# Attention heads on two-bank PSUM tiles, with 1/sum multiplied into the output

## The chip, the core and the metric

The kernel runs on one core of a Trainium2 chip. Its engines, each with its own in-order instruction stream, are named as the profile names them: PE (TensorE: matmuls; PEld is its weight loads), DVE (VectorE), ACT (ScalarE), POOL (GpSimd) and SP (SyncE, whose queue issues the weight loads). The metric is the device time of one execution in microseconds, the median of several runs; lower is better.

## The reference

A block stack of depth 2 on 256 latent tokens and 256 context tokens, width 1024, in float32. Each layer is: half a feed-forward, a mixer, half a feed-forward, each with an RMS norm that is modulated (scaled, shifted, and gated on its output) by vectors computed from a conditioning vector. Layer 0's mixer is a short convolution, layer 1's is attention with 8 query heads over 2 key/value heads; only the latent tokens attend, to all 512 tokens. Cut to what matters here:

```python
def _attend(q, k, v):
    s = jnp.einsum('bqhgd,bkhd->bhgqk', q, k).astype(jnp.float32) * (ATTN_HEAD_DIM ** -0.5)
    p = jax.nn.softmax(s, axis=-1).astype(v.dtype)
    return jnp.einsum('bhgqk,bkhd->bqhgd', p, v)

def reference(...):
    lat, cx = x, ctx
    for i in range(DEPTH):
        ...
        mod = (jax.nn.silu(c) @ mod_w[i] + mod_b[i]).reshape(bsz, 3, 3, 1, D_MODEL)
        modc = (jax.nn.silu(c_ctx) @ mod_w[i] + mod_b[i]).reshape(3, 3, D_MODEL)
        lat = lat + 0.5 * mod[:, 0, 2] * _swiglu(_modulate(lat, norm_g[i, 0], mod[:, 0, 0], mod[:, 0, 1]), ffn_w13[i, 0], ffn_w2[i, 0])
        ...
            y, yc = _gqa_mixer(h, hc, ctx_out, attn_w_qkv[j], attn_q_g[j], attn_k_g[j], attn_w_o[j], cos, sin)
        ...
        lat = lat + mod[:, 1, 2] * y
        ...
    return lat
```

## The kernel before

**Exactness.** A float32 product is made of three matmuls: every operand is split into a high part that TensorE takes at full rate and a low rest. `split` is two instructions, a copy to the high part on ACT (L98) and a subtraction for the low part on DVE (L99), and `mm3` issues high x high, high x low and low x high (L122, L123, L124). So every weight tile of 128x1024 costs one ACT copy, called wh in the profile, and one DVE subtraction, wl.

**Layout and stages.** Activations lie with the channels on the 128 partitions and 512 tokens along the free axis. The stages run in this order: a feed-forward, the convolution, a feed-forward (layer 0); a feed-forward, the attention, a feed-forward (layer 1). The first three feed-forwards work on all 512 tokens and make their hidden tiles in block pairs: `Pair` forms a 2x2 block product with seven products instead of eight (`head`, `five`, `six`, `seven`, `four`), from sums of weight blocks that DVE forms and splits. There are 54 such pairs. The last feed-forward has 256 tokens only and no pairs. Each is followed by projections (`project`) with the second weight matrix.

**Modulation.** Besides the first two, the modulation vectors are computed on DVE: 224 units, each one custom instruction (L142, output called junk) that multiplies 128x1024 weights with the conditioning vector and sums, and a short read of the accumulator. The weights come in loads of 1 MB (modT) into the three buffers wr that all weights share, through SP's queue. `tick(n)` releases n more units at that place of the program; `mod_ready` forces those that are due. Ticks of 6 stand in each step of the convolution, smaller ones in the projections, and 2 for each head.

**Attention.** After the projections of q and k with norm and rotary embedding, `v_proj(0..3)` make v for four tiles of 128 tokens. Then, for each of 8 heads: `scores` (two query tiles of 128, each in a PSUM bank of its own, psc: three matmuls of 512 columns, a maximum over the row on DVE L1042, its scaled negative nb L1044, the exponential e on ACT L1050 that sums into sm, the reciprocal r L1054, and the scaled probabilities pn = e * r on GpSimd L1058); `turn` (eight transposes on TensorE L1067 into two banks pt, each split to pth and ptl); `mix` (12 matmuls into pav, then the split to a). PSUM has eight banks: two pools, psm with six and pss with two, are open for the whole kernel.

The heads are written two ahead:

```python
    pns, pts = {0: scores(0)}, {}
    v_proj(2)
    v_proj(3)
    pns[1] = scores(1)
    for hd in range(HEADS):
        if hd + 2 < HEADS:
            pns[hd + 2] = scores(hd + 2)
        pts[hd] = turn(pns.pop(hd))
        if hd:
            mix(hd - 1, pts.pop(hd - 1))
        tick(2)
    mix(HEADS - 1, pts.pop(HEADS - 1))
```

Then wo is projected (py, 192 matmuls of 256 columns), finished into x (L446) with squares and sums for the next norm, and the last feed-forward begins (first matmul pg). Between them stand the norm's sums ss (L237, L248), ri (L246), t (L256) and hh (L266).

**What sets the order.** A scheduler places all instructions when the program is built: it may move them within an engine's stream against the written order, by its own priorities. On the chip the order on each engine is fixed, and each instruction waits for the semaphores of what it reads or overwrites.

Of the kernel before, what the change touches and what calls it, by code (L numbers as in the profile page):

```python
# [16 lines left out]
P = 128  # L17
# [24 lines left out]
def hybrid_kernel(ctx: ExitStack, tc: tile.TileContext, a: dict, out: bass.AP):  # L42
# [7 lines left out]
    psm = ctx.enter_context(tc.tile_pool(name="psm", bufs=6, space=bass.MemoryType.PSUM))  # L50
    pss = ctx.enter_context(tc.tile_pool(name="pss", bufs=2, space=bass.MemoryType.PSUM))
# [8 lines left out]
    def psum(s="ps"):  # L60
        return psm.tile([P, T2], F32, tag="mm", name=nm(s))

    def psmall(s="pq"):
        return pss.tile([P, T2], F32, tag="sm", name=nm(s))
# [468 lines left out]
    class Pair:  # L533
# [66 lines left out]
        def seven(self):  # L600
            self.prod(self.p, "S3", "T3", False)
            nc.vector.tensor_tensor(
                out=self.u[:, S:], in0=self.p, in1=self.gm[:, S:], op=ALU.add
            )

# [232 lines left out]
    for m in range(KT):  # L838
# [36 lines left out]
        tick(6)  # L875
# [29 lines left out]
    pqs = pss.tile([P, T2], F32, tag="sm", name="pqs")  # L905
# [126 lines left out]

    def scores(hd):
        kv = hd // (HEADS // KVH)
        r_ = []
        for qt in range(2):
            o = (hd % 2) * S + qt * P
            ps = psum("psc")
            mm3(ps, tuple(t[:, o : o + P] for t in qs[hd // 2]), ks[kv], True, True)
            ci = hd * 2 + qt  # L1040
            mx = ap.tile([P, 1], F32, name=nm("mx"), tag="mx", bufs=4)
            nc.vector.reduce_max(mx, ps, axis=AX.X)  # L1042
            nb = ap.tile([P, 1], F32, name=nm("nb"), tag="nb", bufs=4)
            nc.vector.tensor_scalar(  # L1044
                out=nb, in0=mx, scalar1=scq[:, ci : ci + 1], scalar2=-1.0,
                op0=ALU.mult, op1=ALU.mult,
            )
            e = tp.tile([P, T2], F32, name=nm("e"), tag="sg", bufs=3)
            sm = ap.tile([P, 1], F32, name=nm("sm"), tag="smx", bufs=4)
            nc.scalar.activation(  # L1050
                out=e, in_=ps, func=AF.Exp, scale=scq[:, ci : ci + 1], bias=nb, accum_out=sm
            )
            r = ap.tile([P, 1], F32, name=nm("r"), tag="r", bufs=4)
            nc.vector.reciprocal(r, sm)  # L1054
            if qt == 0:
                pn2 = hot("pn", F32)
            pn = pn2[:, qt * T2 : qt * T2 + T2]
            nc.gpsimd.tensor_scalar(out=pn, in0=e, scalar1=r, scalar2=None, op0=ALU.mult)  # L1058
            r_.append(pn)
        return r_  # L1060

    def turn(pn):
        pth, ptl = (hot(t).rearrange("p (b q) -> p b q", q=S) for t in ("pth", "ptl"))
        for qt in range(2):
            pt = psum("pt")
            for kt in range(4):
                nc.tensor.transpose(  # L1067
                    pt[:, kt * P : kt * P + P], pn[qt][:, kt * P : kt * P + P], ident
                )
            split(  # L1070
                pth[:, :, qt * P : qt * P + P], ptl[:, :, qt * P : qt * P + P],
                pt.rearrange("p (k q) -> p k q", k=4),
            )
        return pth, ptl
# [3 lines left out]
    def mix(hd, pt):  # L1078
# [4 lines left out]
        po = psum("pav")  # L1083
        for kt in range(4):
            vw = tuple(t[:, kv * P : kv * P + P] for t in vs[kt])
            mm3(po[:, :S], vw, (pt[0][:, kt, :], pt[1][:, kt, :]), kt == 0, kt == 3)
        o = (hd % 2) * S
        ah, al = (t[:, o : o + S] for t in at[-1])
        split(ah, al, po[:, :S])
        aos.append((ah, al))  # L1090

    pns, pts = {0: scores(0)}, {}
    v_proj(2)
    v_proj(3)
# [99 lines left out]
```

## Time and profile before

| | us |
|---|---|
| time, median of 3 runs (lowest to highest) | 1596.06 (1595.92 to 1598.62) |
| span of the profiled execution | 1599.4 |
| PE busy | 1572.9 (98%) |
| DVE busy | 1304.2 (82%) |
| ACT busy | 718.6 (45%) |
| POOL busy | 29.7 (2%) |

The profiled execution has no time of its own beside its span. The span is 3.3 us over the median of the runs. Busy times are of one execution; a wait is put down to the semaphore that came last.

### The profile page before, as it was taken

To read this page: it belongs to the slowest core of one execution; us is meant where nothing else is said; L and a number is where in the kernel's file an instruction comes from. 1 tells how busy PE (TensorE), PEld (TensorE's weight loads), DVE (VectorE), ACT (ScalarE), POOL (GpSimd) and SP (SyncE) were. 2 spreads that over 40 slices of the span, in tenths; PEclk is the share of its full clock that TensorE was granted. 3 is DMA by queue.
4 is the path that set the end of the run, shared out by engine and by line. 5 is a ranking of instruction groups with operands and counts; after the bars stand their busy time and mean duration, and the time that the engine had idled before them with its cause. 6 is when DMAs were issued, how large, how long until landed. Compare 5 with 4: busy or idle time off the path is not lost.

```text
span 1599.4 us, 25805 instructions
## 1 busy us (share of the span) xinstructions
PE 1572.9 (98%) x10674; PEld 1452.2 (91%) x10674; DVE 1304.2 (82%) x1984; ACT 718.6 (45%) x1103; POOL 29.7 (2%) x20
## 2 busy tenths in 40 slices
PE   8999999999999999999999999999999998899999
PEld 6788998998888899999899899889899897899999
DVE  4778788879998879799798899898797799965554
ACT  5632452544322366335245375245254455554443
POOL 0000000000000000000000000000000005100000
PEclk9999999999999999999999999999999999989999
DMA  8455234234565422453443423452432554755462
GB/s 312 173 185 187 103 106 175 103 117 160 184 220 198 162 80 83 155 185 100 139 145 106 174 78 108 175 191 96 155 132 97 181 199 150 261 189 187 167 201 104
DMA packets 38422, 248.79 MB, mean 156 GB/s; under 512 B 5280, under 2 KB 7072, under 8 KB 12448
## 3 DMA queue, kind: packets, MB, share of 16 engines
q1 hardware_dynamic: 35712, 245.38, 44.0%
q10 hardware_dynamic: 2592, 1.76, 0.4%
q8 instruction: 83, 1.36, 0.3%
q14 instruction: 35, 0.29, 0.1%
HBM read 244.77 MB, written 1.05 MB: 154 GB/s over the span
## 4 chain that ended last, share of the span: by engine, by line
PE 87%; DVE 7%; DMA 3%; ACT 1%; issue 1%; POOL 0%; DVEq 0%; ACTq 0%; SPq 0%; POOLq 0%
PE py L122 8%; PE py L123 8%; PE py L124 8%; PE p L123 6%; PE p L122 6%; PE p L124 6%; PE q L124 5%; PE q L122 5%; PE q L123 5%; PE pg L122 3%; PE pg L123 3%; PE pg L124 3%; PE pu L124 3%; PE pu L123 3%; PE pu L122 3%; DVE junk L142 2%
## 5 line engine op out<-in xcount | busy, mean ns | idle before, releaser
L98 ACT ACTIVATE wh<-wr 128x1024 fp32r<-128x1024 f32 (+2 forms) x276 | 276.4, 1014 | 401.1 <-PE py L123 111.3
L99 DVE TENSOR_TENSOR wl<-wr,wh 128x1024 fp32r<-128x1024 f32 (+2 forms) x276 | 320.0, 1167 | 96.5 <-ACT wh L98 95.9
L142 DVE CUSTOM_DVE_ANT_0 junk<-wr,scbc,modb 128x1024 bf16<-128x1024 f32 x224 | 287.0, 1281 | 38.9 <-DMA wr<-in_modT 36.3
L122 PE MATMUL py<-gh,wh 128*128 128x512 f32 (+1 forms) x746 | 263.2, 353 | 0.0
L123 PE MATMUL py<-gl,wh 128*128 128x512 f32 (+1 forms) x746 | 263.1, 353 | 0.0
L124 PE MATMUL py<-gh,wl 128*128 128x512 f32 (+1 forms) x746 | 262.8, 352 | 0.0
L124 PEld LDWEIGHTS py<-gh,wl 128*128 128x128 f32 x746 | 141.1, 189 | 19.1
L122 PEld LDWEIGHTS py<-gh,wh 128*128 128x128 f32 x746 | 141.2, 189 | 18.5
L123 PEld LDWEIGHTS py<-gl,wh 128*128 128x128 f32 x746 | 141.2, 189 | 18.1
L99 DVE TENSOR_TENSOR wl<-ws,wh 128x1024 fp32r<-128x1024 f32 x108 | 131.8, 1224 | 29.1 <-ACT wh L98 28.9
L98 ACT ACTIVATE wh<-ws 128x1024 fp32r<-128x1024 f32 x108 | 113.5, 1058 | 68.0 <-PE p L123 35.5
L124 PE MATMUL p<-th,wl 128*128 128x256 f32 x432 | 122.2, 283 | 0.0
L123 PE MATMUL p<-tl,wh 128*128 128x256 f32 x432 | 122.2, 283 | 0.0
L122 PE MATMUL p<-th,wh 128*128 128x256 f32 x432 | 122.2, 283 | 0.0
L446 DVE SCALAR_TENSOR_TENSOR x<-py,G,x 128x256 f32<-128x256 f32 x168 | 74.1, 479 | 21.9 <-PE py L124 21.4
L122 PE MATMUL q<-bh,wh 128*128 128x256 f32 x320 | 90.6, 283 | 0.0
L123 PE MATMUL q<-bl,wh 128*128 128x256 f32 x320 | 90.6, 283 | 0.0
L124 PE MATMUL q<-bh,wl 128*128 128x256 f32 x320 | 90.6, 283 | 0.0
L122 PEld LDWEIGHTS p<-th,wh 128*128 128x128 f32 x432 | 82.9, 192 | 0.3
L123 PEld LDWEIGHTS p<-tl,wh 128*128 128x128 f32 x432 | 82.9, 192 | 0.3
L124 PEld LDWEIGHTS p<-th,wl 128*128 128x128 f32 x432 | 82.9, 192 | 0.0
L122 PE MATMUL pg<-hh,wh 128*128 128x256 f32 (+1 forms) x240 | 77.2, 322 | 3.7 <-ACT hh L266 3.6
(238 smaller groups left out, 4049.7 us busy)
## 6 DMA issues: line engine op xcount, KB each, us to landing
wr<-in_w SPq DMA_DIRECT2D x88, 1024.0 KB, 4.9
wr<-in_modT SPq DMA_DIRECT2D x64, 1024.0 KB, 4.9
wr<-in_w2b SPq DMA_DIRECT2D x32, 896.0 KB, 4.6
wr<-in_w2a SPq DMA_DIRECT2D x16, 1024.0 KB, 4.9
wr<-in_mod SPq DMA_DIRECT2D x8, 1024.0 KB, 6.7
wr<-in_cw_cx SPq DMA_DIRECT2D x8, 1024.0 KB, 5.0
wr<-in_cw_b SPq DMA_DIRECT2D x4, 1024.0 KB, 4.9
wr<-in_cw_out SPq DMA_DIRECT2D x4, 1024.0 KB, 4.9
```

The lines of the kernel that those rows point to most:

```text
L98: nc.scalar.activation(out=hi, in_=src, func=AF.Copy)
L99: nc.vector.tensor_tensor(out=lo, in0=src, in1=hi.bitcast(F32), op=ALU.subtract)
L122: nc.tensor.matmul(ps, wh, mh, start=first, stop=False, **kw)
L123: nc.tensor.matmul(ps, wh, ml, start=False, stop=False, **kw)
L124: nc.tensor.matmul(ps, wl, mh, start=False, stop=last, **kw)
L142: nc.vector.tensor_tensor_reduce(out=junk, in0=raw[:, j * D : j * D + D], in1=scbc[:, v, :], scale=1.0, scalar=modb[:, l, col : col + 1], ...
L446: nc.vector.scalar_tensor_tensor(out=x[:, m, s * S : s * S + S], in0=ps[:, o : o + S], scalar=g[:, m, s : s + 1], in1=x[:, m, s * S : s * ...
```

## The change

The PSUM pools are closed for the heads and opened again behind them: for the heads there are two buffers of two banks for scores (psc), one of two banks for the turned probabilities (ptp), and two of one bank for the mixed output (pav). Both query tiles of a head lie in one two-bank tile, so that the maximum, nb, and the reciprocal are one instruction each for a head; the exponentials stay two, for their scale and bias differ. All four `v_proj` stand ahead of the heads, and two scores are made before the first turn.

The exponentials are turned as they are. 1/sum is spread over the partitions by two matmuls with the identity into the free half of the output's bank, copied by ACT to rb, and multiplied by DVE into the output, which is then split. GpSimd has no part in it. The low part of the turned tile is one subtraction of 1024 columns.

The tick of 2 at each head goes; `Pair.seven` gets a tick of 0.5, and the convolution's tick of 6 becomes 5.5.

```diff
--- before.py
+++ after.py
@@ -47,8 +47,20 @@
     hop = ctx.enter_context(tc.tile_pool(name="hop", bufs=16))
     gp = ctx.enter_context(tc.tile_pool(name="gp", bufs=8))
     tp = ctx.enter_context(tc.tile_pool(name="tp", bufs=2))
-    psm = ctx.enter_context(tc.tile_pool(name="psm", bufs=6, space=bass.MemoryType.PSUM))
-    pss = ctx.enter_context(tc.tile_pool(name="pss", bufs=2, space=bass.MemoryType.PSUM))
+    banks = {}
+    stage = ExitStack()
+
+    def use_banks(*pools):
+        stage.close()
+        for name, bufs in pools:
+            banks[name] = stage.enter_context(
+                tc.tile_pool(
+                    name=name, bufs=bufs, space=bass.MemoryType.PSUM, reuse_waits="tile"
+                )
+            )
+
+    use_banks(("psm", 6), ("pss", 2))
+    ctx.callback(stage.close)
     mp = ctx.enter_context(tc.tile_pool(name="mp", bufs=2))
 
     uid = [0]
@@ -58,10 +70,10 @@
         return f"{s}{uid[0]}"
 
     def psum(s="ps"):
-        return psm.tile([P, T2], F32, tag="mm", name=nm(s))
+        return banks["psm"].tile([P, T2], F32, tag="mm", name=nm(s))
 
     def psmall(s="pq"):
-        return pss.tile([P, T2], F32, tag="sm", name=nm(s))
+        return banks["pss"].tile([P, T2], F32, tag="sm", name=nm(s))
 
     def cload(key, shape, eng=None):
         t = const.tile(list(shape), F32, name=key, tag=key)
@@ -602,6 +614,7 @@
             nc.vector.tensor_tensor(
                 out=self.u[:, S:], in0=self.p, in1=self.gm[:, S:], op=ALU.add
             )
+            tick(0.5)
 
         def four(self, g):
             self.prod(self.p, "A22", "T4", False)
@@ -872,7 +885,7 @@
         nc.vector.tensor_tensor(out=z, in0=d, in1=pb, op=ALU.mult)
         zs.append(new_pair("z"))
         split(zs[m][0], zs[m][1], z)
-        tick(6)
+        tick(5.5)
 
     def by_pairs(key):
         box = {}
@@ -902,7 +915,7 @@
     ap = ctx.enter_context(tc.tile_pool(name="ap", bufs=2))
 
 
-    pqs = pss.tile([P, T2], F32, tag="sm", name="pqs")
+    pqs = psmall("pqs")
 
     def sums(ps, c):
         sq = tp.tile([P, T2], F32, name=nm("sq"), tag="gm", bufs=3)
@@ -1030,78 +1043,87 @@
     )
     v_proj(1)
 
+    v_proj(2)
+    v_proj(3)
+    use_banks(("psc", 2), ("ptp", 1), ("pav", 2))
+
+    def double(pool, s):
+        return banks[pool].tile([P, 2, T2], F32, tag="t", name=nm(s))
+
     def scores(hd):
         kv = hd // (HEADS // KVH)
-        r_ = []
+        ps = double("psc", "psc")
         for qt in range(2):
             o = (hd % 2) * S + qt * P
-            ps = psum("psc")
-            mm3(ps, tuple(t[:, o : o + P] for t in qs[hd // 2]), ks[kv], True, True)
-            ci = hd * 2 + qt
-            mx = ap.tile([P, 1], F32, name=nm("mx"), tag="mx", bufs=4)
-            nc.vector.reduce_max(mx, ps, axis=AX.X)
-            nb = ap.tile([P, 1], F32, name=nm("nb"), tag="nb", bufs=4)
-            nc.vector.tensor_scalar(
-                out=nb, in0=mx, scalar1=scq[:, ci : ci + 1], scalar2=-1.0,
-                op0=ALU.mult, op1=ALU.mult,
-            )
-            e = tp.tile([P, T2], F32, name=nm("e"), tag="sg", bufs=3)
-            sm = ap.tile([P, 1], F32, name=nm("sm"), tag="smx", bufs=4)
+            mm3(ps[:, qt, :], tuple(t[:, o : o + P] for t in qs[hd // 2]), ks[kv], True, True)
+        sc = scq[:, 2 * hd : 2 * hd + 2]
+        mx = ap.tile([P, 2], F32, name=nm("mx"), tag="mx", bufs=3)
+        nc.vector.reduce_max(mx, ps, axis=AX.X)
+        nb = ap.tile([P, 2], F32, name=nm("nb"), tag="nb", bufs=3)
+        nc.vector.scalar_tensor_tensor(
+            out=nb, in0=mx, scalar=-1.0, in1=sc, op0=ALU.mult, op1=ALU.mult
+        )
+        e = hot("e", F32)
+        sm = ap.tile([P, 2], F32, name=nm("sm"), tag="smx", bufs=3)
+        for qt in range(2):
             nc.scalar.activation(
-                out=e, in_=ps, func=AF.Exp, scale=scq[:, ci : ci + 1], bias=nb, accum_out=sm
-            )
-            r = ap.tile([P, 1], F32, name=nm("r"), tag="r", bufs=4)
-            nc.vector.reciprocal(r, sm)
-            if qt == 0:
-                pn2 = hot("pn", F32)
-            pn = pn2[:, qt * T2 : qt * T2 + T2]
-            nc.gpsimd.tensor_scalar(out=pn, in0=e, scalar1=r, scalar2=None, op0=ALU.mult)
-            r_.append(pn)
-        return r_
-
-    def turn(pn):
-        pth, ptl = (hot(t).rearrange("p (b q) -> p b q", q=S) for t in ("pth", "ptl"))
-        for qt in range(2):
-            pt = psum("pt")
-            for kt in range(4):
+                out=e[:, qt * T2 : qt * T2 + T2], in_=ps[:, qt, :], func=AF.Exp,
+                scale=sc[:, qt : qt + 1], bias=nb[:, qt : qt + 1],
+                accum_out=sm[:, qt : qt + 1],
+            )
+        r = ap.tile([P, 2], F32, name=nm("r"), tag="r", bufs=4)
+        nc.vector.reciprocal(r, sm)
+        return e, r
+
+    def turn(e):
+        hi, lo = hot("pth"), hot("ptl")
+        pt = double("ptp", "pt").rearrange("p a t -> p (a t)")
+        for kt in range(4):
+            for qt in range(2):
+                o = kt * S + qt * P
                 nc.tensor.transpose(
-                    pt[:, kt * P : kt * P + P], pn[qt][:, kt * P : kt * P + P], ident
+                    pt[:, o : o + P], e[:, qt * T2 + kt * P : qt * T2 + kt * P + P], ident
                 )
-            split(
-                pth[:, :, qt * P : qt * P + P], ptl[:, :, qt * P : qt * P + P],
-                pt.rearrange("p (k q) -> p k q", k=4),
-            )
-        return pth, ptl
+        for c in (slice(0, T2), slice(T2, 1024)):
+            nc.scalar.activation(out=hi[:, c], in_=pt[:, c], func=AF.Copy)
+        nc.vector.tensor_tensor(out=lo, in0=pt, in1=hi.bitcast(F32), op=ALU.subtract)
+        return hi, lo
 
     aos, at = [], []
 
-    def mix(hd, pt):
+    def mix(hd, pt, r):
         kv = hd // (HEADS // KVH)
         if hd % 2 == 0:
             t = hot("a")
             at.append((t[:, :T2], t[:, T2:]))
-        po = psum("pav")
+        po = banks["pav"].tile([P, T2], F32, tag="t", name=nm("po"))
         for kt in range(4):
             vw = tuple(t[:, kv * P : kv * P + P] for t in vs[kt])
-            mm3(po[:, :S], vw, (pt[0][:, kt, :], pt[1][:, kt, :]), kt == 0, kt == 3)
+            mm3(
+                po[:, :S], vw, tuple(t[:, kt * S : kt * S + S] for t in pt), kt == 0, kt == 3
+            )
+        for qt in range(2):
+            nc.tensor.matmul(
+                po[:, S + qt * P : S + qt * P + P], r[:, qt : qt + 1].to_broadcast([P, P]),
+                ident, start=True, stop=True,
+            )
+        rb = tp.tile([P, S], F32, name=nm("rb"), tag="t", bufs=3)
+        nc.scalar.copy(rb, po[:, S:])
+        nc.vector.tensor_tensor(out=rb, in0=rb, in1=po[:, :S], op=ALU.mult)
         o = (hd % 2) * S
         ah, al = (t[:, o : o + S] for t in at[-1])
-        split(ah, al, po[:, :S])
+        split(ah, al, rb)
         aos.append((ah, al))
 
-    pns, pts = {0: scores(0)}, {}
-    v_proj(2)
-    v_proj(3)
-    pns[1] = scores(1)
+    es, pts = {0: scores(0), 1: scores(1)}, {}
     for hd in range(HEADS):
+        pts[hd] = turn(es[hd][0])
         if hd + 2 < HEADS:
-            pns[hd + 2] = scores(hd + 2)
-        pts[hd] = turn(pns.pop(hd))
+            es[hd + 2] = scores(hd + 2)
         if hd:
-            mix(hd - 1, pts.pop(hd - 1))
-        tick(2)
-    mix(HEADS - 1, pts.pop(HEADS - 1))
-
+            mix(hd - 1, pts.pop(hd - 1), es.pop(hd - 1)[1])
+    mix(HEADS - 1, pts.pop(HEADS - 1), es.pop(HEADS - 1)[1])
+    use_banks(("psm", 6), ("pss", 2))
 
     hn = Plain(S)
     project(
```

More of the change, by code (lines that the diff above doesn't have):

```diff
@@ new lines, in scores @@
+        nc.vector.scalar_tensor_tensor(
[4 more added lines that the diff above has]
+        for qt in range(2):
+            nc.scalar.activation(
+                out=e[:, qt * T2 : qt * T2 + T2], in_=ps[:, qt, :], func=AF.Exp,
+                scale=sc[:, qt : qt + 1], bias=nb[:, qt : qt + 1],
+                accum_out=sm[:, qt : qt + 1],
+            )
```

1 line of the change is left out of this document (removed).

## The prediction

> **What bounds the kernel now.** I read the page first, then busy time by stretches, the waits inside the heads stage, the groups of instructions there, and last the timeline around the heads.
>
> ```profile
> span 1599.4 us, 25805 instructions
> PE 1572.9 (98%) x10674; PEld 1452.2 (91%) x10674; DVE 1304.2 (82%) x1984; ACT 718.6 (45%) x1103; POOL 29.7 (2%) x20
> PE 87%; DVE 7%; DMA 3%; ACT 1%; issue 1%; POOL 0%; DVEq 0%; ACTq 0%; SPq 0%; POOLq 0%
> ```
>
> Over the whole span TensorE is the bound: 98% busy, 87% of the chain. VectorE comes next. That is an average, and the changed stage is short. Columns below: stretch, length, busy PE, PEld, DVE, ACT, POOL (instructions), granted clock, DMA share, GB/s. The first row is the last block pairs and the q, k, v projections; the second the heads; the third the output projection wo.
>
> ```profile
> 1200.00:1326.00 126.00, 125.21 (x879) 116.92 (x878) 103.88 (x176) 60.36 (x98) 0.00 (x0) 1.00 0.48 165
> 1326.00:1376.00 50.00, 43.35 (x291) 38.17 (x290) 47.17 (x109) 30.48 (x65) 29.52 (x16) 0.97 0.40 136
> 1376.00:1400.00 24.00, 20.49 (x165) 19.72 (x163) 22.32 (x40) 10.60 (x18) 0.00 (x0) 0.98 0.92 334
> ```
>
> In the heads TensorE is idle for 6.65 of 50 us, while VectorE is busy for 47.17. So the change can win at most the idle 6.65 us and some clock, and only if VectorE, which is nearly full there, gets out of the way. The waits of the stage (waiter, releaser: total, times, longest):
>
> ```profile
> PE pt L1067 <- POOL pn L1058: 3.0, 3, 2.0
> PE pt L1067 <- DVE ptl L99: 1.4, 2, 1.0
> ACT e L1050 <- DVE nb L1044: 8.5, 6, 2.0
> ```
>
> GpSimd's scaling, which the change deletes, ends only 3.0 us of TensorE's idle time. ScalarE's exponentials wait 8.5 us for VectorE's nb, which stands behind other VectorE work: the stage's second limit is VectorE's queue.
>
> **The change, part by part.** Prices (groups with their busy time and the mean ns of one; the last two rows are of the timeline, with start and length in us):
>
> ```profile
> L1042 DVE TENSOR_REDUCE mx<-psc 128x1 f32<-128x512 f32 x16 | 10.6, 682 | 0.9 <-PE psc L124 0.9
> L99 DVE TENSOR_TENSOR ptl<-pt,pth 128x512 fp32r<-128x512 f32 x16 | 10.3, 678 | 0.0
> L142 DVE CUSTOM_DVE_ANT_0 junk<-wr,scbc,modb 128x1024 bf16<-128x1024 f32 x23 | 29.4, 1278 | 1.1 <-DMA wr<-in_modT 1.0
> L1050 ACT ACTIVATE e<-psc,nb,scq 128x512 f32<-128x512 f32 x16 | 12.4, 776 | 10.1 <-DVE nb L1044 8.5 <-POOL pn L1058 0.9 <-DVE ptl L99 0.8
> L98 ACT ACTIVATE pth<-pt 128x512 fp32r<-128x512 f32 x16 | 9.0, 599 | 0.1
> L99 DVE TENSOR_TENSOR a<-pav,a 128x256 fp32r<-128x256 f32 x8 | 3.3, 417 | 1.2 <-ACT a L98 1.2
> L1044 DVE TENSOR_SCALAR nb<-mx,scq 128x1 f32<-128x1 f32 x16 | 2.9, 205 | 0.0
> L1054 DVE RECIPROCAL r<-sm 128x1 f32<-128x1 f32 x16 | 2.3, 156 | 0.7 <-ACT e L1050 0.6
> 1316.93 1.95 PE L996 MATMUL kri<-ident,rq 128*128 128x128 f32 x16
> 1370.95 2.35 DVE L99 TENSOR_TENSOR wl<-wr,wh 128x1024 fp32r<-128x1024 f32 x2
> ```
>
> *Two-bank tiles.* The 16 maxima, 16 nb, 16 r and 16 ptl become 8 each. No 1024-wide maximum is in the trace; the nearest row is the 1024-wide subtraction, 2.35 us for two, the second starting 1.13 after the first if the last one has the group's length of 1.22 (an estimate from that row). I take 1.13 for mx and ptl; the bounds are 0.68 and twice 0.68. Against two 512-wide ones (1.36 by their means) that is worth 0 to 0.23 us each, 0 to 3.7 over the stage. Halving nb and r drops 8 x (0.205 + 0.156) = 2.9 us of VectorE's time, some of it overlapped.
>
> *Output scaled at the end.* Per head two broadcast matmuls of the kri form are added (eight such calls stand in the trace as 16 records of 1.95 us together, so at most 0.49 per head and 3.9 over eight heads), one ScalarE copy, and one VectorE multiplication, 0.42 like the 256-wide subtraction, 3.3 in all. The multiplication stands in VectorE's queue ahead of the output's split. GpSimd's 16 scalings go.
>
> *Modulation.* The order of instructions in the changed program shows that this part barely happens: between the first maximum and the last output split stand 10 units (12 before), with 208 ahead (203) and 6 behind (9). The scheduler still pulls units into the heads. So VectorE loses there 2 x (1.28 + 0.08), some 2.6 us, which the multiplications take back (3.3). The five units that go ahead come in groups of three or four within 2.5 to 4 pairs:
>
> ```profile
> 303.82 0.43 DVE L602 TENSOR_TENSOR p<-p,gm 128x256 f32<-128x256 f32 x1 [0.57 <-PE p L124]
> 304.79 1.23 DVE L99 TENSOR_TENSOR wl<-ws,wh 128x1024 fp32r<-128x1024 f32 x1 [0.54 <-ACT wh L98]
> 306.23 1.23 DVE L99 TENSOR_TENSOR wl<-ws,wh 128x1024 fp32r<-128x1024 f32 x1 [0.22 <-ACT wh L98]
> 310.82 0.28 PE L122 MATMUL q<-th,wh 128*128 128x256 f32 x1
> ```
>
> A pair leaves VectorE 0.57 + 0.54 + 0.22 = 1.33 us idle, and the split that ends at 306.03 is used by TensorE at 310.82, 4.8 us later. A unit of 1.36 fits; I cost them at nothing, and 5 x 1.36 = 6.8 if that cover were gone. Their 1 MB loads move with them past the weight loads on SP's queue: DMA is at 0.48 before the heads, 0.92 in the wo stage, so three loads leave a full stretch for a half-empty one. Zero to some tenths of gain.
>
> *The start of the heads.* This is the largest term, and a new wait. Timeline of before:
>
> ```profile
> 1327.17 0.68 DVE L1042 TENSOR_REDUCE mx<-psc 128x1 f32<-128x512 f32 x1
> 1327.53 1.28 ACT L1050 ACT_TABLE_LOAD   x1
> 1332.47 0.40 PE L122 MATMUL psc<-kh,qh 128*128 128x512 f32 x1
> 1332.70 0.40 PE L123 MATMUL psc<-kl,qh 128*128 128x512 f32 x1
> 1335.22 0.60 PE L1067 MATMUL pt<-ident,pn 128*128 128x128 f32 x4
> 1340.80 0.96 PE L1067 MATMUL pt<-ident,pn 128*128 128x128 f32 x4 [1.95 <-POOL pn L1058]
> 1343.79 0.41 PE L122 MATMUL pav<-pth,vh 128*128 128x256 f32 x1
> 1344.56 0.28 PE L123 MATMUL pav<-ptl,vh 128*128 128x256 f32 x1
> 1345.72 1.03 PE L1067 MATMUL pt<-ident,pn 128*128 128x128 f32 x8
> ```
>
> Before, scores(0) runs amid the v projections; its maxima, the table load and its exponentials lie under v_proj(2) and v_proj(3), and turn(0) starts at 1335.22 with no wait. After, TensorE runs all four v projections and then scores(0), scores(1). Matmuls of 512 columns start 0.23 apart (1332.47, 1332.70). Take the 6 of scores(0), 1.4 us, out of the time to 1332.47: the projections end at 1331.1. scores(0) must then wait for the eviction of v_proj(3), which has the same bank: a 256-wide copy (about 0.4, under the 0.6 of the 512-wide pth) and a subtraction (0.42) with some 0.3 of hand-overs, 1332.2 to 1332.7. Two scores take 2.75: 1335.4. VectorE's order is mx0, mx1, nb0, nb1: nb0 waits behind mx1, until 1335.4 + 1.13 + 0.2 = 1336.9 with hand-over. In the changed order the table load waits for nb0 (before, it began at 1327.53, with the maximum at work until 1327.85): + 1.28, then two exponentials, 1.55, and hand-over: turn(0) starts at 1340.3 instead of 1335.22. TensorE has nothing else in that gap, since scores(2) is queued behind turn(0). **+5.1 us.** Bounds: 3.0 if the eviction is quick and the table load comes early, 6.5 if the splits of wo now ahead of mx0 are late.
>
> *From turn(0) to the last mix.* The last mix of before ends, and wo goes on, here:
>
> ```profile
> 1370.11 0.28 PE L122 MATMUL py<-a,wh 128*128 128x256 f32 x1
> 1371.91 0.28 PE L122 MATMUL py<-a,wh 128*128 128x256 f32 x1
> 1396.04 0.28 PE L124 MATMUL py<-a,wl 128*128 128x256 f32 x1
> ```
>
> Before: 1371.91 - 1335.22 = 36.7 us. After, TensorE needs from turn(0) only eight turnings of 0.8 (eight transposes last 1.03 to the end of the last one, 0.8 to the next start), six scores of 1.4, eight mixes of 12 x 0.12 = 1.44 (0.12 is the wo stretch's 20.49 us over 165 matmuls) and eight times 0.49 for 1/sum: 30.2 us. VectorE, in its written order from ptl0 (which follows turn(0) by 0.8 and two copies of 0.5 to 0.6, so 1342.4): eight ptl 9.0, six mx 6.8, eight units 10.9 (two are ahead), six nb and six r 2.2 at most, sixteen 256-wide operations 6.7, in all 35.6. Neighbours overlap (two wl last 2.35, not 2 x 1.22); at 0.06 for each of 50 instructions that is 32.5. That gives 1374.9 to 1378.0. There is one two-bank buffer for turned probabilities, so turn(k+1) waits for ptl(k): a chain of 0.8 + 1.1 + 1.13 with hand-overs, 3.3 us, shorter than VectorE's 4.1 to 4.5 per head; it closes no ring of its own but places short waits. The last mix comes after ptl7: I set its end at 1378.0, between 1375 and 1380. 37.7 instead of 36.7: **+1.0 us** (-2 to +3). VectorE takes over the bound that the start-up wait doesn't; the 6.65 us of idle TensorE time isn't won.
>
> *wo and the step to the last feed-forward.* Before, ten of wo's 192 matmuls were in by 1371.91 (the first at 1370.11), and the rest took 24.2 us, of which 182 x 0.12 = 21.8 is work. After, all 192 come behind the last mix, 23.0, with two of wo's splits done ahead: **-1.2 us** (-2 to +1).
>
> ```profile
> 1397.66 1.28 DVE L142 CUSTOM_DVE_ANT_0 junk<-wr,scbc,modb 128x1024 bf16<-128x1024 f32 x1
> 1399.18 1.23 DVE L99 TENSOR_TENSOR wl<-wr,wh 128x1024 fp32r<-128x1024 f32 x1
> 1400.39 1.20 DVE L99 TENSOR_TENSOR wl<-wr,wh 128x1024 fp32r<-128x1024 f32 x1
> 1402.86 0.58 PE L122 MATMUL pg<-hh,wh 128*128 128x256 f32 x1 [1.11 <-ACT hh L266]
> 1409.00 0.41 PE L122 MATMUL pg<-hh,wh 128*128 128x256 f32 x1
> ```
>
> Between wo's end and the first pg, 6.7 us, VectorE's queue holds a unit and two weight splits between the last x and t. In the changed order one split is left there: a unit and a split less, 1.28 + 1.2: **-2.4 us** (-2.5 to 0, if the unit only hid a DMA).
>
> *The granted clock.* After its 1.95 us wait TensorE's matmuls of 0.28 take 0.41 until about 1344.4, and again to 1409.0: half clock, 1.7 us lost in the first place. The new gap of some 5 us will bring such a stretch for turn(0), scores(2), scores(3); VectorE's queue then hides part: **+1.0 us** (0 to 3). [...]
>
> Sum: 5.1 + 1.0 - 1.2 - 2.4 + 1.0 = **+3.5 us**, on the profiled execution 1599.4 + 3.5 = 1602.9. That span is 3.3 above the runs' median of 1596.06; the same difference on the median gives **1599.6 us**. A measurement here tells about 0.2%, 3.2 us, from no change (faster is below 1592.9, slower above 1599.3), so the forecast lies just on the slow side.
>
> **The rivals.**
>
> *Faster.* TensorE, not VectorE, ends the heads: units wait in gaps, VectorE's starts overlap, and the stage takes TensorE's own 30.2 from 1340.3, ending at 1370.5 instead of 1378.0. 3.5 - 7.5 = -4.0: 1592.1. For it: VectorE has gaps to fill while turn(0) waits. Against: 10 units are still in its written order, and 47.17 of 50 before.
>
> *Cancelled.* The table load or the eviction comes 2 us earlier and the heads end 1.5 us earlier: 3.5 - 3.5 = 0: 1596.1. For it: each is within its bounds.
>
> *Slower still.* The pairs become VectorE's: a group of four units is 5.4 us in 2.5 to 4 pairs that leave 3.3 to 5.3 idle. It decides where the 4.8 us lead of a split is used up; then each of five units costs its 1.36: +6.8, 1606.4. Against: two pairs without units restore the lead.
>
> *The change doesn't do what it says* holds for the modulation in part, and stands in the sum.
>
> **How the numbers follow.** Forecast 0.45 (its own range 1596 to 1603; 0.33 of it beyond the bound on the slow side, 0.12 within), faster 0.28, cancelled 0.15, slower still 0.12. So faster 0.28, same 0.15 + 0.12 = 0.27, slower 0.33 + 0.12 = 0.45. The range runs from 1590.5, just under the faster rival, to 1606, near the slower one.
>
> **What would show it.** In the profile after: POOL empty in the heads; TensorE idle by 4 to 5 us ahead of turn(0), released by e; a table load behind nb0; VectorE over 90% busy from then, TensorE below 85%; ten units there; the first pg some 4.3 us behind wo's end; pairs of unchanged length. Wrong would be: turn(0) by 1337, last mix before 1372, or pairs that differ by over 0.05 us each.

## The result, and the profile after

The changed kernel takes 1602.24 us in the median of 20 runs (1599.27 to 1606.07), the kernel before 1597.93 (1595.14 to 1604.17): a ratio of 1.0025, 95% interval 1.0016 to 1.0034. It is slower by 0.25%, some 4.0 us (the two medians lie 4.3 apart); +3.5 was forecast.

The page of the changed kernel, its span and busy times:

```profile
span 1597.6 us, 25806 instructions
PE 1570.5 (98%) x10706; PEld 1452.3 (91%) x10706; DVE 1302.8 (82%) x1960; ACT 722.4 (45%) x1111; POOL 0.2 (0%) x4
```

This span is 1.8 us shorter than that of before, although the kernel is slower: the profiled execution took 1599.4 us, one of the quickest of its 20. It lies 1.8 us over its span; with the same difference that of before took some 1601 (an estimate), one of the slower ones. Whole spans can't be compared to 4 us; stretches can. The kernel before was therefore profiled a second time (e8 below). Three stretches, cut at the start of v_proj(0), of turn(0), of wo's first matmul behind the last mix, and of the last feed-forward's first matmul. First before, then after (length, busy PE, PEld, DVE, ACT, POOL, clock, DMA share, GB/s):

```profile
1318.63:1335.22 16.59, 16.59 (x125) 15.79 (x124) 15.23 (x34) 7.09 (x15) 3.27 (x2) 1.00 0.59 206
1335.22:1371.91 36.69, 30.04 (x196) 25.68 (x194) 33.86 (x80) 24.79 (x55) 26.25 (x15) 0.95 0.39 138
1371.91:1402.86 30.95, 25.80 (x202) 24.62 (x200) 29.07 (x50) 13.37 (x23) 0.00 (x0) 0.94 0.84 302
```

```profile
1312.66:1333.76 21.10, 15.64 (x119) 14.61 (x117) 19.00 (x31) 9.55 (x17) 0.00 (x0) 1.00 0.55 202
1333.76:1373.07 39.31, 33.41 (x228) 29.76 (x229) 32.79 (x61) 24.83 (x60) 0.00 (x0) 0.96 0.36 122
1373.07:1402.46 29.39, 26.00 (x207) 25.36 (x205) 19.58 (x33) 14.86 (x24) 0.00 (x0) 0.94 0.54 187
```

Up to turn(0): +4.51. From there to the last mix: +2.62. wo and the step to the feed-forward: -1.56. Together +5.57; the last feed-forward then takes 195.1 us instead of 196.5. Sum: +4.2 against a measured +4.0. With e8 in the place of before (85.4 us to the last feed-forward, then 196.0) it is +3.5.

The shorter last feed-forward is not work saved. TensorE starts it at half clock, and before does so for longer (first before, then after, each from the first pg to the end of the half clock):

```profile
1402.86:1409.29 6.43, 6.43 (x29) 6.29 (x30) 6.43 (x15) 3.80 (x8) 0.00 (x0) 0.50 0.45 181
1402.46:1405.60 3.14, 3.14 (x14) 3.14 (x15) 3.14 (x9) 2.06 (x5) 0.00 (x0) 0.50 0.22 89
```

Half of each is lost, 3.2 and 1.6 us (an estimate from the clock of 0.50). In all 14 profiles the last feed-forward takes 194.8 to 196.5 us; without that half it takes 193.1 to 193.6.

The start, in the timeline of the changed kernel (start, length, engine, and in brackets the idle time before and its releaser):

```profile
1326.79 2.35 DVE L111 TENSOR_TENSOR wl<-wr,wh 128x1024 fp32r<-128x1024 f32 x2
1327.01 0.47 PE L134 MATMUL psc<-kh,qh 128*128 128x512 f32 x1 [1.72 <-DVE vl L111]
1329.05 2.35 DVE L1061 TENSOR_REDUCE mx<-psc 128x2 f32<-128x1024 f32 x2
1331.32 0.28 DVE L1063 SCALAR_TENSOR_TENSOR nb<-mx,scq 128x2 f32<-128x2 f32 x2
1331.55 1.28 ACT L1069 ACT_TABLE_LOAD   x1 [4.58 <-DVE nb L1063]
1332.84 0.78 ACT L1069 ACTIVATE e<-psc,nb,scq 128x512 f32<-128x512 f32 x1
1333.76 0.37 PE L1084 MATMUL pt<-ident,e 128*128 128x128 f32 x1 [3.74 <-ACT e L1069]
```

TensorE idles for 1.72 us, then for 3.74. Read the VectorE rows: the two maxima begin the moment the two splits of wo are done, nb comes behind both maxima, and the table load behind nb. The last matmul of scores(0) ends at 1328.64, that of scores(1) at 1330.02, and the second maximum starts at 1330.19; so without the two splits nb could come only some 0.2 us earlier. The 1024-wide maximum, which no trace had shown, costs what the 1024-wide subtraction costs: 2.35 for two.

The waits from turn(0) to the last mix, after:

```profile
PE pt L1084 <- DVE ptl L1089: 3.7, 4, 1.3
PE po L135 <- DVE ptl L1089: 1.3, 1, 1.3
PE psc L134 <- ACT e L1069: 0.5, 1, 0.5
```

GpSimd's 3.0 us of waits are gone; 3.7 us for the one turning buffer stand in their place.

### The profile page after: what moved, and what is told of

It is laid out like the page before. It is cut to its first block, busy times and chain, and to the rows that moved or that the text cites. A ratio compares the mean times of both kernels' runs of the same rounds, so it can differ in the third digit from the quotient of the medians.

```text
span 1597.6 us, 25806 instructions
## 1 busy us (share of the span) xinstructions
PE 1570.5 (98%) x10706; PEld 1452.3 (91%) x10706; DVE 1302.8 (82%) x1960; ACT 722.4 (45%) x1111; POOL 0.2 (0%) x4
## 5 line engine op out<-in xcount | busy, mean ns | idle before, releaser
L134 PEld LDWEIGHTS py<-gh,wh 128*128 128x128 f32 x746 | 141.2, 189 | 18.3
```

The lines of the kernel that those rows point to most:

```text
L134: nc.tensor.matmul(ps, wh, mh, start=first, stop=False, **kw)
```

## The experiments

Ratios are to the kernel before, with their 95% interval. In the table, the stretches of one profiled execution of each: from v_proj(0) to turn(0), from turn(0) to the last matmul of the last mix, both together, and from v_proj(0) to the first matmul of the last feed-forward.

| kernel | ratio | to turn(0) | to last mix | sum | to feed-forward |
|---|---|---|---|---|---|
| before | 1 | 16.6 | 36.6 | 53.2 | 84.2 |
| before again (e8) | 0.9992 (0.9980 to 1.0005) | 16.6 | 36.6 | 53.2 | 85.4 |
| changed | 1.0025 (1.0016 to 1.0034) | 21.1 | 39.3 | 60.4 | 89.8 |
| e1 | 0.9998 (0.9985 to 1.0011) | 15.3 | 38.4 | 53.7 | 83.1 |
| e2 | 1.0009 (0.9994 to 1.0023) | 19.8 | 37.4 | 57.2 | 86.1 |
| e3 | 1.0003 (0.9990 to 1.0015) | 19.8 | 38.1 | 57.9 | 86.5 |
| e4 | 0.9966 (0.9952 to 0.9980) | 16.6 | 35.1 | 51.7 | 80.4 |
| e5 | 0.9946 (0.9934 to 0.9958) | 16.6 | 33.8 | 50.4 | 79.2 |
| e6 | 0.9951 (0.9935 to 0.9966) | 16.6 | 32.4 | 49.0 | 77.1 |
| e7 | 0.9967 (0.9956 to 0.9978) | 15.3 | 36.1 | 51.4 | 80.2 |
| e9 | 0.9940 (0.9923 to 0.9957) | 16.6 | 32.3 | 48.9 | 77.0 |
| e10 | 0.9961 (0.9948 to 0.9974) | 15.3 | 36.0 | 51.3 | 79.5 |
| e11 | 0.9970 (0.9958 to 0.9982) | 16.6 | 36.4 | 53.0 | 82.8 |
| e12 | 1.0027 (1.0015 to 1.0038) | 21.1 | 39.3 | 60.4 | 89.9 |

**e8, the kernel before once more.**

> The kernel before, unchanged: how far one profiled execution differs from another in each stretch. Expected: the same within 0.3 us from v_proj(0)'s first matmul to the last mix and to the first matmul of the last feed-forward; the differences lie in the first 60 us, where the first loads land. If the last feed-forward again takes 196.5 us, its 1.4 to 1.6 us less in the changed kernel and in the modulation-only kernel is an effect of the edits; if it comes out at 195, it is chance.

To the last mix the two profiles agree within 0.1 us. To the last feed-forward they differ by 1.2 us, not by the 0.3 expected, nearly all of it in the step behind wo; the last feed-forward is at 196.0. So the last stretches can be read to about 1 us, and the heads to a tenth where the granted clock is the same, as it is in these two (0.95).

**e1, v projections among the scores.**

```diff
-    v_proj(2)
-    v_proj(3)
     use_banks(("psc", 2), ("ptp", 1), ("pav", 2))
...
-    es, pts = {0: scores(0), 1: scores(1)}, {}
+    es, pts = {0: scores(0)}, {}
+    v_proj(2, "pav")
+    v_proj(3, "pav")
+    es[1] = scores(1)
```

> The changed kernel with v_proj(2) and v_proj(3) put back between scores(0) and scores(1); their output takes the two one-bank buffers of the mixed output. Theory A (the start of the heads is the loss: TensorE idles 1.7 us for the eviction and 3.7 us for the first exponentials): turn(0) starts about 4 us earlier counted from the first matmul of v_proj(0), the last mix ends 3 to 4 us earlier, the time falls by 3 to 4 us against the changed kernel, to about the kernel before (ratio to before 1.000). Theory B (VectorE's queue sets the length of the heads whatever the start): turn(0) comes earlier but the last mix ends at most 1.5 us earlier, ratio to before 1.0015 or more.

Theory A: turn(0) comes 5.8 us earlier, the last mix 6.7, more than it said, and the ratio is 0.9998. Taking the start-up away takes away as much as the whole loss. It isn't the only such cost: e2 and e3 each win part of it too.

**e3, the table load early, and e12, another bank for scores(0).**

```diff
     inv_rms(0, 16)
+    warm = ap.tile([P, 1], F32, name="warm", tag="warm", bufs=1)
+    nc.scalar.activation(out=warm, in_=rms[:, :1], func=AF.Exp, scale=-1.0)
```

> The changed kernel with a one-element exponential issued on ScalarE right behind the square root of the q norm, so that the table load runs under the v projections and not behind the first nb. Theory A: turn(0) starts 1.3 us earlier, the time falls by about 1 us (ratio to before about 1.0018). Theory B (VectorE's queue, with two units ahead of the first ptl, absorbs it): turn(0) earlier, the last mix not, no change of the time (1.0025).

```diff
-    use_banks(("psc", 2), ("ptp", 1), ("pav", 2))
+    use_banks(("pav", 2), ("ptp", 1), ("psc", 2))
```

> The changed kernel with the pools of the heads opened in the order mixed output, turning, scores, so that scores(0) lies in banks of which v_proj(2) had the last, not v_proj(3); all else, the order of instructions too, is the same. Theory A (the wait of 1.72 us for the eviction of v_proj(3) is a cost of the shared bank): that wait goes, turn(0) stands 19.4 us behind the first matmul of v_proj(0) instead of 21.1, the last mix comes 1 to 1.7 us earlier, ratio to before 1.0005 to 1.002. Theory B (VectorE, which has splits of wo behind that eviction, gives the time back): turn(0) within 0.5 us of 21.1, ratio 1.002 to 1.003.

e3: turn(0) comes 1.3 us earlier, as Theory A said, the last mix even 2.5; the ratio of 1.0003 (to 1.0015) is a larger gain than A's 1.0018. e12 is Theory B's: scores(0) still starts behind an eviction, now that of v_proj(2), which stands right ahead of v_proj(3)'s in VectorE's queue. TensorE's idle time falls only from 1.72 to 1.29, and nothing else moves. The timeline of e12:

```profile
1328.64 0.50 PE L134 MATMUL psc<-kh,qh 128*128 128x512 f32 x1 [1.29 <-DVE vl L111]
1328.83 2.35 DVE L111 TENSOR_TENSOR wl<-wr,wh 128x1024 fp32r<-128x1024 f32 x2
1331.10 2.35 DVE L1061 TENSOR_REDUCE mx<-psc 128x2 f32<-128x1024 f32 x2
1335.81 0.43 PE L1084 MATMUL pt<-ident,e 128*128 128x128 f32 x1 [4.14 <-ACT e L1069]
```

What scores(0) gains, the first exponential's wait loses (4.14 instead of 3.74), for the maxima begin behind the splits of wo in any case. So the shared bank alone isn't what costs: with it gone, the splits hold the maxima. What the splits cost alone was not tried; by the times in the timeline of the changed kernel it is some 0.2 us, for nb stands behind the second maximum and that behind scores(1). The bulk of the start-up is this order itself: all v projections, two scores, two maxima, nb, table load and exponential, one behind the other.

**e2, no units in the heads.**

```diff
-            tick(0.5)
+            tick(0.85)
```

> The changed kernel with a tick of 0.85 in place of 0.5 in every pair: in the built order all 224 units stand ahead of the first maximum, none in the heads (10 in the changed kernel) and none behind. Theory A (VectorE is the bound from turn(0) on): the stretch from turn(0) to the last mix, 39.4 us in the changed kernel, falls to 31 to 34; the pairs hide the 16 units; the time falls by 5 to 8 us, ratio to before 0.997 to 0.9995. Theory B (the pairs have no room): the 16 units cost up to 1.36 each, +22 us there, ratio to before above 1.005. Theory C (dependences, not VectorE's fullness, set the heads): the stretch falls by less than 2 us.

Theory C, just: without a single unit there the stretch falls by 1.9 us, and Theory A's 31 to 34 us are refuted. In its profile, first the stretch, then a stretch of pairs; below them TensorE's waits from turn(0) on:

```profile
1334.00:1371.00 37.00, 32.84 (x225) 29.20 (x226) 23.29 (x42) 24.53 (x60) 0.00 (x0) 0.95 0.00 1
1116.90:1216.90 100.00, 100.00 (x686) 93.38 (x685) 91.66 (x130) 42.54 (x63) 0.00 (x0) 1.00 0.53 188
```

```profile
PE pt L1084 <- ACT e L1069: 2.8, 2, 2.4
PE pt L1084 <- DVE nb L1063: 1.8, 2, 0.9
PE pt L1084 <- DVE ptl L1089: 1.2, 1, 1.2
```

VectorE is busy for 23.29 of 37 us and the stage is hardly shorter: how full VectorE was did not bound it. TensorE is busy for 32.84, of which half clock makes about 1.9 (an estimate: a granted clock of 0.95 over 37 us), and waits for single evictions and exponentials. In the pairs TensorE is busy for 100.00 of 100 us with VectorE at 91.66, and it runs 686 matmuls in them, as before and the changed kernel do in the like stretch: 16 more units ahead of the heads cost nothing there.

**e4, the modulation part alone, on the kernel before.**

```diff
+            tick(0.5)      # Pair.seven
...
-        tick(6)
+        tick(5.5)
...
             mix(hd - 1, pts.pop(hd - 1))
-        tick(2)
```

> The kernel before with the modulation part of the change alone (no tick at the heads, 0.5 in each pair, 5.5 in the convolution): heads, banks and GpSimd as before. In the built order 8 units stand in the heads (12 before), 206 ahead (203), 10 behind (9). Theory A (VectorE is nearly the bound of the heads before): 4 units of 1.36 fewer shorten the heads by 2 to 4 us, ratio to before 0.9975 to 0.999. Theory B (GpSimd's scalings and the waits between engines set them): less than 1 us, ratio 0.9995 to 1.0005. If the pairs paid for the units: above 1.001.

It is faster by 0.34%, more than either theory said (Theory A's 0.9975 lies within the interval). The heads give 1.5 us; the table shows 3.8 us up to the last feed-forward, which itself takes 194.9 us instead of 196.5, for it starts with 3.0 us of half clock instead of 6.4.

**e5, the second part added to e4: 1/sum in the output, one-bank tiles.**

```diff
-            nc.gpsimd.tensor_scalar(out=pn, in0=e, scalar1=r, scalar2=None, op0=ALU.mult)
...
+        for qt in range(2):
+            nc.tensor.matmul(
+                po[:, S + qt * P : S + qt * P + P], er[qt][1].to_broadcast([P, P]),
+                ident, start=True, stop=True,
+            )
+        rb = tp.tile([P, S], F32, name=nm("rb"), tag="t", bufs=3)
+        nc.scalar.copy(rb, po[:, S:])
+        nc.vector.tensor_tensor(out=rb, in0=rb, in1=po[:, :S], op=ALU.mult)
```

> The modulation-only kernel with the second part of the change added: the exponentials are turned unscaled, 1/sum is spread by two matmuls per head, copied, and multiplied into the output; GpSimd idle; one-bank tiles and the order of the v projections as before. Theory A (TensorE is the heads' scarce engine): eight times 0.36 us of matmuls are added, 2.9, and GpSimd's waits of 2.7 us go, so the stretch from turn(0) to the last mix stays within 1.5 us of 35.0, ratio to before 0.996 to 0.9985. Theory B (GpSimd's scaling was what the heads waited for): the stretch falls by 2.5 us or more, ratio to before below 0.9955.

The stretch falls by 1.3 us, within Theory A's bound, but the ratio, 0.9946, is Theory B's. The stretch of e4, then that of e5, and below them TensorE's waits in e5:

```profile
1328.00:1363.00 35.00, 29.14 (x191) 25.15 (x190) 30.99 (x75) 22.02 (x51) 24.01 (x14) 0.95 0.33 116
1331.90:1365.80 33.90, 31.68 (x227) 27.55 (x225) 31.82 (x82) 24.10 (x58) 0.00 (x0) 1.00 0.35 122
```

```profile
PE pav L122 <- ACT pth L98: 0.8, 2, 0.6
PE pav L122 <- DVE ptl L99: 0.8, 1, 0.8
PE pt L1066 <- DVE ptl L99: 0.3, 1, 0.3
```

TensorE is busy for longer (31.68 against 29.14; the two matmuls of 1/sum, on unsplit operands of 128 columns, take 0.36 us per head, while those of the split operands, of 256 columns, start 0.12 apart), yet the stretch is shorter: it waits for 2 us in all, and with no wait above 0.9 us the granted clock stays at 1.00. So with units in the heads GpSimd's scaling cost more than the list of waits puts to it (3.0 us before, 2.7 in e4): half clock followed, some 1.7 us more (an estimate from the clock of 0.95). e6 shows the limit of this.

**e6 and e9, no units in the heads, without and with 1/sum in the output.** e6 is e4, and e9 is e5, with one more edit:

```diff
-            tick(0.5)
+            tick(0.85)
```

> The modulation-only kernel with 0.85 in place of 0.5 in each pair: all 224 units ahead of the heads, none in them or behind, GpSimd and banks as before. Theory A (VectorE's units still delay the heads): the stretch from turn(0) to the last mix falls from 35.0 to 31 to 33.5, ratio to before 0.994 to 0.996. Theory C (GpSimd, 16 scalings of 1.86 us, and the waits between engines hold it): within 1 us of 35.0, ratio 0.996 to 0.998. If the pairs have no room for 18 more units: above 1.000.

> The scale-only kernel (one-bank tiles, v projections as before, 1/sum in the output) with all 224 units ahead of the heads (0.85 in each pair). Theory A (the one-bank heads end on TensorE once GpSimd and the units are gone): 30.5 to 32.5 us from turn(0) to the last mix (33.8 with 8 units), ratio to before 0.9925 to 0.9945. Theory C (waits between the engines hold it): within 0.7 us of 33.8, ratio 0.994 to 0.996.

Theory A in e6 (32.4) and in e9 (32.3). Taking out the last units wins 2.7 us in e6, 1.5 in e9. In e6 the clock is back at 1.00, with GpSimd still at work and 1.9 us of waits for it, so most of its 2.7 us may be half clock that didn't come. The ratios of e5, e6 and e9 lie within each other's intervals: once no units stand in the heads, 1/sum in the output wins nothing that these runs could tell from noise. e9 is the quickest in the median (1589.17 us, 0.60% less than before), but not clearly ahead of e5. The pairs take the units without loss again. The stretch of e6, then that of e9, whose heads have TensorE busy for 31.08 of 32.30 us:

```profile
1336.50:1368.80 32.30, 28.03 (x191) 23.86 (x190) 25.39 (x65) 22.07 (x51) 22.29 (x14) 1.00 0.09 33
1333.37:1365.67 32.30, 31.08 (x224) 27.63 (x223) 27.22 (x71) 23.72 (x58) 0.00 (x0) 1.00 0.10 34
```

**e11, the v projections first, with one-bank tiles,** on e5:

```diff
-    pns, pts = {0: scores(0)}, {}
     v_proj(2)
     v_proj(3)
+    pns, pts = {0: scores(0)}, {}
```

> The scale-only kernel with v_proj(2) and v_proj(3) ahead of scores(0), as in the changed kernel, but with the six one-bank buffers open throughout. Theory A (the order of the v projections costs by itself, for maxima, table load and exponentials lose their cover): turn(0) 18.5 to 20 us behind the first matmul of v_proj(0) instead of 16.6, ratio to before 0.9955 to 0.997. Theory F (only the bank shared with v_proj(3) and the nb behind two 1024-wide maxima cost): turn(0) within 1 us of 16.6, ratio 0.994 to 0.9953.

Neither theory had the place of the cost right. turn(0) still stands at 16.6, because here a free bank lets scores(2) run ahead of it; the wait comes behind it (timeline, then the stretch from turn(0)):

```profile
1338.50 0.36 PE L122 MATMUL pav<-pth,vh 128*128 128x256 f32 x1 [2.11 <-DVE ptl L99]
```

```profile
1331.99:1368.39 36.40, 32.92 (x225) 29.00 (x225) 33.62 (x85) 24.69 (x60) 0.00 (x0) 0.95 0.28 97
```

The ratio is Theory A's, on the edge of its range: 0.9970 against 0.9946 in e5, a cost of 2.6 us in the heads, of a wait and the half clock behind it.

**e7, all three repairs, and e10, the turning in halves as well.** e7 has the edits of e1, e2 and e3 together; e10 adds the diff below.

> The changed kernel with all three repairs together: v_proj(2), v_proj(3) between scores(0) and scores(1), the early table load, all units ahead of the heads. Theory A (start of the heads plus VectorE): turn(0) at 14 to 16 us behind the first matmul of v_proj(0) (21.1 in the changed kernel), the last mix 33 to 36 us behind turn(0), ratio to before 0.994 to 0.997. Theory C (the 2.9 us of matmuls for 1/sum and the waits of the single turning buffer stay): 36 to 38 us behind turn(0), ratio 0.997 to 0.9995.

```diff
-    use_banks(("psc", 2), ("ptp", 1), ("pav", 2))
+    use_banks(("psc", 2), ("ptp", 2), ("pav", 2))
...
+        for k2 in range(2):
+            pt = banks["ptp"].tile([P, T2], F32, tag="t", name=nm("pt"))
...
+            c = slice(k2 * T2, k2 * T2 + T2)
+            split(hi[:, c], lo[:, c], pt)
```

> The changed kernel with the three repairs, and the two banks of the turning used as two one-bank buffers: four transposes, one copy and one subtraction for each, so that one half can be turned while the other is read. Theory D (the single two-bank turning buffer is the ring that holds the heads): 36.1 us from turn(0) to the last mix fall to 32.5 to 34, ratio to before 0.994 to 0.9955. Theory E (the two score buffers of two banks, held until both exponentials are read, or the half-filled start hold it): 35 us or more, ratio 0.9955 to 0.998.

e7 makes the changed heads faster than before: the ratio of 0.9967 is Theory A's, the 36.1 us behind turn(0) are just Theory C's. But up to the last mix it stays 2.5 us longer than e9, which has one-bank tiles and is otherwise alike but for what the number of buffers asks of the order (turn ahead of the scores two heads on) and the early table load. Its stretch, and TensorE's waits in it:

```profile
1331.80:1367.90 36.10, 31.49 (x228) 28.17 (x227) 25.84 (x46) 24.25 (x59) 0.00 (x0) 1.00 0.13 46
```

```profile
PE psc L134 <- ACT e L1069: 2.1, 1, 2.1
PE pt L1084 <- DVE ptl L1089: 2.0, 3, 1.0
PE po L135 <- DVE ptl L1089: 0.6, 1, 0.6
```

e10 takes the wait for the turning buffer from 2.0 to 0.7 us and wins nothing clear, in the stretch or in the ratio (Theory E):

```profile
1336.02:1372.02 36.00, 32.98 (x230) 29.67 (x228) 26.03 (x53) 24.15 (x59) 0.00 (x0) 0.95 0.12 45
```

```profile
PE psc L134 <- ACT e L1069: 2.1, 1, 2.1
PE pt L1085 <- DVE ptl L111: 0.7, 2, 0.4
```

The wait for a score buffer stays at 2.1, and here half clock stands in the stretch (0.95, TensorE busy 32.98 instead of 31.49), which hides what the shorter waits may have won in this one profile. The ratios of the two kernels, 0.9967 and 0.9961, lie within each other's intervals. Whether more score buffers would close the gap to e9 was not tried: the heads' pools (two buffers of two banks for scores, two banks for turning, two for the mixed output) already take as many banks, eight, as the six and two of the kernel before.

## Why the prediction was right or wrong

The sign, the size and the range were right: +3.5 forecast, +4.0 measured. That the sum came so close is luck. Its largest term (the start) and that of wo were right in the main. The other three were not, one change was not in the sum at all, and what the terms were off by nearly cancels: about -0.6 (start), +1.6 (turn(0) to the last mix), +2.0 (step to the feed-forward), -1.0 (clock) and -1.4 us (last feed-forward).

The parts of the change also have larger effects than their sum. One part after another is put on the kernel before: modulation -0.34% (e4), 1/sum in the output to -0.54% (e5), the v projections first to -0.30% (e11), and the two-bank tiles with their pools to +0.25% (changed kernel). So two parts win and two lose; the step from e11 to the changed kernel costs 0.55%, 7.0 us of it in the column to the feed-forward (82.8 to 89.8). That step isn't the tiles alone: the order of turn and scores goes with them, and 10 units stand in the changed heads, 6 in those of e11. e7 against e9, both without units, is the cleaner pair: 0.9967 and 0.9940, 2.5 us to the last mix.

*The start of the heads, +5.1:* measured +4.5, and the mechanism was right: TensorE idles ahead of turn(0) until the first exponential, with the table load behind nb, and e1 shows that taking it away takes away the loss. Inside the term two errors partly cancel. nb0 was put 18.3 us behind v_proj(0), and came at 18.7 (the terms given add up to 18.1). From there two exponentials were counted, but turn(0) starts behind the first one alone, 0.8 us sooner. The wait for the shared bank, part of the sum, is worth nothing by itself: e12 shortens it without effect.

*From turn(0) to the last mix, +1.0:* measured +2.6, and the reason failed. The step "VectorE takes over the bound" is refuted by e2: with VectorE busy for 23 us instead of 33 the stretch falls by 1.9 us only. TensorE's own time was mis-sized: 30.2 us, measured 33.4, of which the clock of 0.96 over 39.3 us makes 1.6 (an estimate). The single turning buffer, of which the prediction said that it "closes no ring of its own but places short waits", was given no price for these waits: TensorE waited 3.7 us for it, and 1.3 us more for a ptl that the mix reads. That VectorE would be over 90% busy is wrong too: 32.79 of 39.31, 83%. The ten units in the heads came as said.

*The modulation, "barely happens":* wrong as a price. It moves few units, but e4 alone wins 0.34%, some 5.4 us. Four units fewer in the heads give 1.5 us there. Another 2.3 us lie between the last mix and the last feed-forward, where one profile can't be read closer than 1 us. The last 1.6 us are the half clock at the start of the last feed-forward, which stays 3.4 us shorter. Why fewer units in the heads end it sooner is not shown.

*GpSimd's scaling, 3.0 us of waits:* too low with units in the heads, where half clock followed (0.95 before and in e4); without units (e6) it did not.

*wo, -1.2:* right; the last mix to wo's last matmul fell from 24.2 to 23.0. But only four of wo's matmuls stood ahead of the last mix, not ten, so what went is mostly waits.

*The step to the feed-forward, -2.4:* from 6.8 to 6.4 us. A unit and a split did leave VectorE's queue, but the queue wasn't what held this step. VectorE now waits there, 0.85 us for rs and 1.32 us for TensorE's ss, and TensorE waits 1.33 us for acc: the chain of the norm through the engines remains. A second profile of before has 7.9 us, so it may be -1.5.

*The clock, +1.0:* half clock came behind the new gap as forecast, from 1333.9 to 1337.3, but before has a stretch of the same length (1341.0 to 1344.4), which the term did not take off. 0.95 before, 0.96 after: no cost in the heads. What did change, the half clock at the start of the last feed-forward (-1.4 us there), was not in the sum.

*The pairs, 0:* right, by e2, e6 and e9.

The rival that the pairs become VectorE's is refuted by e2's pair row. The faster rival had the right bound (TensorE) for the wrong kernel: with one-bank tiles, in e9, TensorE is busy for 31.08 of 32.30 us.

On the clock: before, a wait of 1.95 us was followed by half clock; in e7 one of 2.05 us was not (clock 1.00). So the length of a wait alone doesn't decide here. In the profiles of before and of the changed kernel all stretches of half clock (0.50) begin whole multiples of 3.413 us apart: before at 30.30, 40.54, 576.43, 1341.02 and 1399.04 us (0, 3, 160, 384 and 401 steps behind the first), after at 36.86, 1333.92, 1398.78 and 1596.75 (0, 380, 399 and 457 steps). They last one such step, those at 1399.04 and 1398.78 three and two; the one at 1596.75 lasts to the end of the span. The steps of e7, taken to be as long, are counted back from the end of the half clock in its last feed-forward, where its matmuls start 0.12 apart again instead of 0.21 (about 1400.4, 20 steps behind 1332.13). Cut into these steps, the wait of before lies within one, which leaves TensorE idle for 2.07 us, and the next step runs at half clock; that of e7 (1334.26 to 1336.31) is divided between two steps, which leave it idle for 1.29 and 1.33 us. First before, then e7:

```profile
1337.61:1341.02 3.41, 1.34 (x9) 0.68 (x8) 3.41 (x9) 2.08 (x5) 3.41 (x3) 1.00 0.00 0
1341.02:1344.43 3.41, 3.41 (x16) 3.19 (x14) 3.09 (x8) 2.47 (x6) 3.41 (x2) 0.50 0.15 19
1332.13:1335.54 3.41, 2.12 (x13) 1.52 (x11) 3.41 (x5) 0.91 (x3) 0.00 (x0) 1.00 0.42 144
1335.54:1338.95 3.41, 2.08 (x10) 1.58 (x11) 2.13 (x5) 3.21 (x8) 0.00 (x0) 1.00 0.78 291
```

In e10, with a wait of 2.1 us for an exponential, as in e7, half clock stands in the stretch (0.95). The idle time within a step doesn't settle it either: before, a step with 0.98 us of it (573.02 to 576.43) was followed by half clock; after, one with 1.72 us (1323.68 to 1327.09) was not. What decides is not shown.

## What to carry to other kernels

Read what stands in the queue ahead of the first instruction of a new stage: work that lay hidden beside another stage (maxima, a table load, the first exponentials) becomes the start-up when the order is made tidier. A wider tile that merges two instructions into one also merges two buffers into one; here it saved VectorE time that wasn't scarce (busy for 25.84 us in e7, 27.22 in e9) and cost TensorE waits that were (4.7 us against 1.1; which of the buffers costs most is not shown). Try the parts of a combined change one at a time: here two of them win 0.5% and the other two take it back and more. Before you explain a microsecond or two between two profiles, compare the granted clock of the two stretches.

## What was not expected of the hardware

A whole-span comparison of one execution each was off by 6 us: the spans said -1.8, the medians +4.3. From the convolution's last matmul into pc to v_proj(0) the profiled executions took 794.3 to 802.7 us; three kernels that are alike up to the heads but for the scheduler's order near them (e2, e7, e10) took 797.2, 799.6 and 802.7, while a 100 us stretch of pure pairs shows TensorE busy for 100.00 in e2 (from 1116.90) and in e10 (from 1118.00). The granted clock goes with most of it: on the way there half clock stands for 0 us in e4 (794.3), 3.4 in e2 and 10.2 in e10 (by the clocks of 0.98 in one 100 us stretch of e2, 0.97 and 0.98 in two of e10), of which half is lost (an estimate from the clock of 0.50). First e4, then e10, in the first 100 us of it:

```profile
517.10:617.10 100.00, 98.73 (x668) 91.53 (x667) 86.54 (x133) 52.23 (x81) 0.00 (x0) 1.00 0.33 116
518.00:618.00 100.00, 96.52 (x625) 89.14 (x624) 82.00 (x127) 47.65 (x74) 0.00 (x0) 0.97 0.33 116
```

Without that half these three take 794.3, 795.5 and 797.6 us, before (798.9, with 3.4 us of half clock) 797.2, and the changed kernel, with none, 796.7; what makes this rest was not tried.
